# Experts' gate and up rows dealt to the partitions in runs of eight, and a final norm whose factors are computed in groups

## The chip, the cores and the metric

The kernel runs on one core of a Trainium2 chip: TensorE (matmul), VectorE, ScalarE, GpSimd, SyncE (which here only issues transfers) and 16 DMA engines. The metric is the time of one launch on the device, in microseconds (us), as the median of several runs. The profile's short names are PE (TensorE; PEld its weight loads), DVE (VectorE), ACT (ScalarE), POOL (GpSimd) and SP (SyncE); a q behind a name (SPq) is that engine's queue of transfers.

## The reference

One decoder layer over 1024 tokens of width 1024, all in float32: two kinds of attention side by side, a cross-attention into 256 memory tokens, a mixture of 32 experts, a final norm. What matters here is the last third:

```python
def _rms_norm(x, gain):
    y = xf * lax.rsqrt(jnp.mean(xf * xf, axis=-1, keepdims=True) + RMS_EPS)
    return y * gain

def _hierarchical_moe(h, ...):          # h = _rms_norm(x, norm_ffn_g), 1024 x 1024
    # top-1 of 4 groups, then top-2 of its 8 experts, for each token: 2048 assignments
    def block_fn(args):                 # a block of tokens of one expert e
        tok, wt, e = args
        xb = h_pad[tok]
        hidden = jax.nn.silu(xb @ w_gate[e]) * (xb @ w_up[e])   # 1024 -> 256
        return (hidden @ w_down[e]) * wt[:, None]               # 256 -> 1024
    ...
x = x + _hierarchical_moe(...)
return _rms_norm(x, norm_final_g)
```

`w_gate` and `w_up` are [32, 1024, 256], `w_down` is [32, 256, 1024]: an expert has 1 MB of each.

## The kernel before

**The order.** The program's operations are recorded and set in order by a list scheduler written in the kernel (`Sched`), which estimates each operation's cost, gives buffers out and emits one instruction list for each engine before anything runs. All recorded operations are emitted from one place, so nearly every row of the profile carries L481, and rows are told apart by the names of their tiles. Most tiles of 4 KB a partition come from one pool of 50 buffers (`t4`).

**The tokens.** For each of eight tiles of 128 tokens `r_keep` multiplies the residual `xr` by the norm's gain `gb` on GpSimd into `xn`, scales it by the token's factor on ScalarE, and stores it to `XN` in HBM; the residual itself goes to `ACC`. Routing (`r_top`, `r_rank`, `r_index`, `r_weights`) then yields for each expert a list of up to 96 tokens, `gidx`.

**The experts.** `experts` runs over the 32 experts. `moe_piece(e, j)` loads one piece of weights into a tile `eraw`: for j = 0 to 3 two rows of 128 of the 1024 input features, gate beside up, in two transfers of 256 KB (two runs of 1 KB for each partition); for j = 4 and 5 128 rows of `w_down` in one of 512 KB. All are issued by SyncE. `m_split` makes of each tile a rounded part `ehi` (ScalarE) and a rest `elo` (VectorE). `m_x` gathers the expert's 96 rows of `XN` on GpSimd's queue (`xg`) and transposes them, eight blocks of 128 features; `m_gu` multiplies (three matmuls for each block of features: high by high, high by low, low by high); `m_h` and `m_d` make the hidden layer and the down product, and an indirect transfer on GpSimd's queue adds the 96 rows to `ACC`. A row of the contraction, partition q of block k, is feature 128 k + q in both the tokens and the weights. Loads are ordered ahead of their use by two experts (`AHEAD`) and as far as free buffers let the scheduler go.

**Overflow.** For an expert with more than 96 tokens there is a loop (`tc.For_i`) behind a branch, with weights `wgu`, `wdn` of its own; in this run it is not entered.

**The final norm.** For each of eight tiles: load 128 rows of `ACC` into `yt`; square and sum on ScalarE (`sq`, into one column of `ss`); twelve operations on VectorE over that one column (`rsqrt_mean`: scale, bit trick, three Newton steps); one VectorE product of the tile with the factor and the gain; store to `out`. The `ss` tiles come from a pool of four.

Of the kernel before, what the change touches and what calls it, by code (L numbers as in the profile page):

```python
# [12 lines left out]
F32 = mybir.dt.float32  # L13
# [3 lines left out]
AF = mybir.ActivationFunctionType  # L17
OP = mybir.AluOpType
# [4 lines left out]
P = 128  # L23
D = 1024
S = 1024
KT = D // P
NT = S // P
# [28 lines left out]
WHOLE_GU = range(0)  # L56
WHOLE_D = range(4)
WHOLE_PV = ()
TAILV = range(8)
PARK = range(8)  # L60
NPRE = 0
NXG = 3
# [10 lines left out]
NS = 96  # L73
# [442 lines left out]
def hybrid_kernel(ctx: ExitStack, tc: tile.TileContext, a, out):  # L516
    nc = Sched(tc.nc)
    ctx.enter_context(tc.manual_schedule())
    mm = nc.tensor.matmul

    def mm3(o, ah, al, bh, bl, start, stop):
        mm(o, ah, bh, start=start, stop=False)
        mm(o, ah, bl, start=False, stop=False)
        mm(o, al, bh, start=False, stop=stop)

    def sb(stack, name, bufs=1, side="left"):
        return nc.pool(stack, tc, name, bufs, side=side, reuse_waits="tile")
# [3 lines left out]
    sm = sb(ctx, "sm")  # L531
# [14 lines left out]
    def t4(name, *shape, dt=F32):  # L546
        v = big.tile(list(shape) or [P, 1024], dt, tag="t4", name=name, bufs=N4)
        if name == "eraw":
            v.tile.reserve = RESERVE_M
        if name in ("ehi", "elo", "xT", "xw", "hid", "hw", "sg", "y"):  # L550
            v.tile.reserve = RESERVE_W
        return v

    def carve(name):

        t, pos = t4(name), [0]

        def take(*shape, dt=F32):
            n = math.prod(shape) * (2 if dt == BF16 else 4) // 4
            v = t[:, pos[0]:pos[0] + n].bitcast(dt)  # L560
            pos[0] += n
            names = "abc"[:len(shape)]
            return v.rearrange(f"p ({' '.join(names)}) -> p {' '.join(names)}",
                               **dict(zip(names[1:], shape[1:]))) if len(shape) > 1 else v

        return take
# [66 lines left out]
    def rsqrt(dst, v, tmp):  # L633

        nc.vector.tensor_scalar(tmp.bitcast(I32), v.bitcast(I32), 1, None, op0=OP.arith_shift_right)
        nc.vector.tensor_scalar(dst.bitcast(I32), tmp.bitcast(I32), -1.0, 1597463007.0, op0=OP.mult, op1=OP.add)
        for _ in range(3):
            nc.vector.tensor_mul(tmp, dst, dst)
            nc.vector.scalar_tensor_tensor(tmp, tmp, -0.5, v, op0=OP.mult, op1=OP.mult)
            nc.vector.scalar_tensor_tensor(dst, tmp, 1.5, dst, op0=OP.add, op1=OP.mult)  # L640

    def rsqrt_mean(dst, ss, n, tmp):

        nc.vector.tensor_scalar(ss, ss, 1.0 / n, EPS, op0=OP.mult, op1=OP.add)
        rsqrt(dst, ss, tmp)
# [506 lines left out]
    xr = {}  # L1152
# [232 lines left out]
    rt = {}  # L1385
# [46 lines left out]
    def r_keep(t):  # L1432

        x = t4("xn")
        nc.gpsimd.tensor_mul(x, xr[t], rt["gb"])
        nc.scalar.activation(x, x, AF.Copy, scale=rs_[t])
        nc.sync.dma_start(XN[t * P:(t + 1) * P], x)
        nc.sync.dma_start(ACC[t * P:(t + 1) * P], xr[t])
# [170 lines left out]
    w_g, w_u, w_d = (a[n].rearrange("o e d f -> (o e) d f") for n in ("w_expert_gate", "w_expert_up", "w_expert_down"))  # L1609
    pieces = {}  # L1610
# [10 lines left out]
    def moe_piece(e, j):  # L1621

        if e >= NE or (e, j) in pieces:
            return
        raw = pieces[e, j] = t4("eraw", P, 2, 512)
        if j < 4:
            for w, o in ((w_g, 0), (w_u, 256)):
                nc.sync.dma_start(raw[:, :, o:o + 256], w[e, j * 256:(j + 1) * 256].rearrange("(k p) f -> p k f", p=P))
        else:
            nc.sync.dma_start(raw.rearrange("p a c -> p (a c)"), w_d[e, (j - 4) * P:(j - 3) * P])  # L1630

    def moe_load(e):
        for j in range(6):
            moe_piece(e, j)
# [30 lines left out]
    def m_gu(e):  # L1665
        gu = bank()
        for k in range(KT):
            x = st[e]["x"][k // 4]
            sl = slice((k % 4) * NS, (k % 4 + 1) * NS)
            if e in WHOLE_GU:  # L1670
                mm(gu[0:NS], x[:, sl], pieces[e, k // 2][:, k % 2], start=k == 0, stop=k == KT - 1)
            else:
                wh, wl = st[e][k // 2]
                mm3(gu[0:NS], x[:, 0, sl], x[:, 1, sl], wh[:, k % 2], wl[:, k % 2], k == 0, k == KT - 1)
        sg = t4("sg")[:, 0:FF]
        nc.scalar.activation(sg[0:NS], gu[0:NS, 0:FF], AF.Silu)
        nc.vector.tensor_mul(sg[0:NS], sg[0:NS], gu[0:NS, FF:2 * FF])
        st[e]["sg"] = sg
# [141 lines left out]
    lazy, nc = nc, tc.nc  # L1820
    mm = nc.tensor.matmul
# [7 lines left out]
    with tc.If(rnov > 0):  # L1829
# [37 lines left out]
        n = 0  # L1867
# [33 lines left out]
        with tc.For_i(0, rnov, 1) as b:  # L1901
            ev = nc.sync.value_load(bei[0:1, bass.ds(b, 1)], min_val=0, max_val=NE - 1)
            ix = take(1, 2, dt=I32)
            nc.vector.tensor_copy(ix, oidx[:, :, bass.ds(b, 1)].rearrange("p a o -> p (a o)"))
            wx = take(1, 1)
            nc.vector.tensor_copy(wx, ow[:, bass.ds(b, 1)])
            wgu = [r4("wgu", P, 2, 512) for _ in range(4)]
            wdn = [r4("wdn") for _ in range(2)]
            for i in range(4):
                for src, o in ((w_g, 0), (w_u, 256)):  # L1910
                    nc.sync.dma_start(wgu[i][:, :, o:o + 256], src[bass.ds(ev, 1), i * 256:(i + 1) * 256].rearrange(
                        "o (k p) f -> p (o k) f", p=P))
            for i in range(2):
                nc.sync.dma_start(wdn[i], w_d[bass.ds(ev, 1), i * P:(i + 1) * P].rearrange("o p f -> p (o f)"))
            xg = r4("oxg")
            nc.vector.memset(xg, 0.0)
            nc.gpsimd.indirect_dma_start(out=xg, out_offset=None, in_=XN_[:, :],
                                         in_offset=bass.IndirectOffsetOnAxis(ap=ix[:, 1:2], axis=0),
                                         bounds_check=S - 1, oob_is_err=False)
            xT = r4("oxT")  # L1920
            for g in range(2):
                xp = rbank()
                for k in range(4):
                    o = (4 * g + k) * P
                    nc.tensor.transpose(xp[:, k * P:(k + 1) * P], xg[:, o:o + P], ident_)
                nc.vector.tensor_copy(xT[:, g * 512:(g + 1) * 512], xp)
            gu = rbank()
            for k in range(KT):
                mm(gu, xT[:, k * P:(k + 1) * P], wgu[k // 2][:, k % 2], start=k == 0, stop=k == KT - 1)
            sg = take(1, FF)  # L1930
            nc.scalar.activation(sg, gu[:, 0:FF], AF.Silu)
            nc.vector.tensor_mul(sg, sg, gu[:, FF:2 * FF])
            hp = rbank()
            for k in range(2):
                nc.tensor.transpose(hp[:, k * P:(k + 1) * P], sg[:, k * P:(k + 1) * P], ident_)
            hT_ = take(1, 2 * P)
            nc.vector.tensor_copy(hT_, hp[:, 0:2 * P])
            y = r4("oy")
            for n in range(2):
                yp = rbank()  # L1940
                for k in range(2):
                    mm(yp, hT_[:, k * P:(k + 1) * P],
                       wdn[k][:, n * 512:(n + 1) * 512], start=k == 0, stop=k == 1)
                nc.vector.tensor_scalar(y[:, n * 512:(n + 1) * 512], yp, wx, None, op0=OP.mult)
            nc.gpsimd.indirect_dma_start(out=ACC_[:, :], out_offset=bass.IndirectOffsetOnAxis(ap=ix[:, 1:2], axis=0), in_=y,
                                         in_offset=None, bounds_check=S - 1, oob_is_err=False, compute_op=OP.add)
    nc = lazy


    gf = t4("gfin")  # L1950
    nc.sync.dma_start(gf, a["norm_final_g"].partition_broadcast(P))
    y_t = ACC.rearrange("(t p) d -> t p d", p=P)
    o_t = out.rearrange("o (t p) d -> (o t) p d", p=P)
    for t in range(NT):
        y, sq = t4("yt"), t4("sq")
        nc.sync.dma_start(y, y_t[t])
        ss = sm.tile([P, 3], F32, name="ss1", bufs=4)
        nc.scalar.activation(sq, y, AF.Square, accum_out=ss[:, 0:1])
        rsqrt_mean(ss[:, 2:3], ss[:, 0:1], D, ss[:, 1:2])
        if t in TAILV:  # L1960
            nc.vector.scalar_tensor_tensor(y, y, ss[:, 2:3], gf, op0=OP.mult, op1=OP.mult)
        else:
            nc.scalar.activation(y, y, AF.Copy, scale=ss[:, 2:3])
            nc.gpsimd.tensor_mul(y, y, gf)
        nc.sync.dma_start(o_t[t], y)


_INS = ["x", "mem", "positions", "norm_mix_g", "w_in", "diff_lambda_q1", "diff_lambda_k1", "diff_lambda_q2",
# [21 lines left out]
```

## Time and profile before

| | |
|---|---|
| median of 3 runs | 1251.87 us (1247.98 to 1252.53) |
| the profiled execution | 1249.66 us, its span 1247.9 us |
| busy in the span | TensorE 1109.2 us (89%), VectorE 890.9 (71%), ScalarE 802.8 (64%), GpSimd 423.8 (34%) |
| DMA | 256.56 MB in 177,883 packets, 131,058 of them under 2 KB; 206 GB/s over the span |
| granted TensorE clock | 0.936 of full speed, mean |

The span is the time from the first to the last instruction; the profiled execution's own time is 1.8 us longer. Times in the views are counted from the start of the span. Attention and cross-attention end near 740 us, routing near 860, the experts' last scatter is issued at 1215.07, and what follows is the final norm. "Idle before" in a row is the time that the engine stood still ahead of the instruction, with the one that released it. A DMA share of 1.0 means that all 16 engines had a packet under way all the time; in some stretches the packets' times add up to a little more than the engines' time, so that packets of one engine overlap.

### The profile page before, as it was taken

To read this page: it belongs to the slowest core of one execution; us is meant where nothing else is said; L and a number is where in the kernel's file an instruction comes from. 1 tells how busy PE (TensorE), PEld (TensorE's weight loads), DVE (VectorE), ACT (ScalarE), POOL (GpSimd) and SP (SyncE) were. 2 spreads that over 40 slices of the span, in tenths; PEclk is the share of its full clock that TensorE was granted. 3 is DMA by queue.
4 is the path that set the end of the run, shared out by engine and by line. 5 is a ranking of instruction groups with operands and counts; after the bars stand their busy time and mean duration, and the time that the engine had idled before them with its cause. 6 is when DMAs were issued, how large, how long until landed. Compare 5 with 4: busy or idle time off the path is not lost. (4 is left out here: it accounts for less than half of the span.)

```text
span 1247.9 us, 19619 instructions
## 1 busy us (share of the span) xinstructions
PE 1109.2 (89%) x6285; PEld 910.3 (73%) x6285; DVE 890.9 (71%) x2100; ACT 802.8 (64%) x1597; POOL 423.8 (34%) x370
## 2 busy tenths in 40 slices
PE   4999999997888899989999999985999988898980
PEld 3988888895667787778899888874676766566650
DVE  5846535468799979989583466787578877777855
ACT  5744326589787778878372455652677877777862
POOL 2214321169545456847311001242143332121110
PEclk9999999999798998889999999985999999989995
DMA  8028899359745553455441142776899999999967
GB/s 294 19 96 312 309 348 246 109 173 266 170 108 120 133 155 84 123 139 186 169 136 35 34 116 75 272 260 223 271 296 285 299 293 317 312 313 323 322 207 276
DMA packets 177883, 256.56 MB, mean 206 GB/s; under 512 B 17035, under 2 KB 131058, under 8 KB 177778
## 3 DMA queue, kind: packets, MB, share of 16 engines
q1 hardware_dynamic: 161728, 208.22, 54.4%
q0 software_dynamic: 15680, 46.75, 12.3%
q8 instruction: 50, 0.82, 0.3%
q14 instruction: 55, 0.45, 0.1%
q10 hardware_dynamic: 370, 0.32, 0.1%
HBM read 208.57 MB, written 55.05 MB: 211 GB/s over the span
## 5 line engine op out<-in xcount | busy, mean ns | idle before, releaser
L481 DVE TENSOR_TENSOR elo<-eraw,ehi 128x1024 fp32r<-128x1024 f32 x184 | 222.9, 1231 | 54.9 <-ACT ehi L481 53.0
L481 ACT CAST ehi<-eraw 128x1024 fp32r<-128x1024 f32 x184 | 189.3, 1050 | 32.6 <-DMA eraw<-in_w_expert_up_dram 23.8
L481 PE MATMUL bank<-ehi,xT 128*96 128x512 f32 x512 | 178.7, 422 | 19.1 <-ACT y L481 18.3
L481 PE MATMUL bank<-k,q 128*128 128x512 f32 (+5 forms) x480 | 131.4, 381 | 19.4 <-ACT pt L481 7.8
L481 PEld LDWEIGHTS bank<-ehi,xT 128*96 128x96 f32 x512 | 88.2, 172 | 59.4 <-ACT y L481 22.8
L481 DVE TENSOR_TENSOR pT<-bank,pT 128x512 fp32r<-128x512 f32 (+2 forms) x208 | 109.6, 560 | 29.7 <-ACT pT L481 28.9
L481 POOL DMA_INDIRECT ACC<-y,gidx x32 | 54.6, 1707 | 210.9 <-ACT y L481 147.8
L481 PE MATMUL acc<-pT,v 128*128 128x512 f32 (+3 forms) x384 | 114.3, 383 | 10.2 <-DVE pT L481 5.4
L481 ACT CAST pT<-bank 128x512 fp32r<-128x512 f32 (+2 forms) x208 | 93.4, 494 | 33.9 <-PE bank L481 33.0
L481 PE MATMUL bank<-hc,pt 128*128 128x128 f32 x640 | 107.8, 295 | 7.8 <-POOL pt L481 3.6
L481 PEld LDWEIGHTS bank<-k,q 128*128 128x128 f32 (+1 forms) x480 | 84.1, 198 | 37.0 <-DVE mx L481 11.5
L481 PE MATMUL bank<-elo,xT 128*96 128x512 f32 x256 | 106.5, 416 | 2.7 <-DVE elo L481 2.4
L481 PEld LDWEIGHTS bank<-hc,pt 128*128 128x128 f32 x640 | 84.8, 153 | 20.1 <-POOL pt L481 4.2
L481 PE MATMUL lbank<-whi,mix 128*128 128x256 f32 x512 | 96.6, 285 | 0.0
L481 PE MATMUL lbank<-whi,hT 128*128 128x256 f32 (+1 forms) x384 | 86.4, 313 | 0.0
L481 PEld LDWEIGHTS acc<-pT,v 128*128 128x128 f32 x384 | 66.1, 197 | 25.7 <-DVE pT L481 11.3
L481 PE MATMUL lbank<-hT,whi 128*128 128x512 f32 x256 | 81.7, 395 | 0.0
L481 PEld LDWEIGHTS lbank<-whi,mix 128*128 128x128 f32 x512 | 81.2, 192 | 0.1
L481 PE MATMUL bank<-ehi,hid 128*96 128x512 f32 x224 | 75.2, 395 | 1.0 <-ACT hid L481 0.8
L481 DVE TENSOR_REDUCE mx<-bank 128x1 f32<-128x512 f32 (+3 forms) x112 | 61.3, 567 | 15.7 <-PE bank L481 15.5
L481 PE MATMUL lbank<-wlo,mix 128*128 128x256 f32 x256 | 72.5, 283 | 0.0
L481 ACT ACTIVATE pt<-bank,mx 128x512 f32<-128x512 f32 (+2 forms) x96 | 55.3, 583 | 19.7 <-DVE mx L481 18.9
(622 smaller groups left out, 2686.6 us busy)
## 6 DMA issues: line engine op xcount, KB each, us to landing
eraw<-in_w_expert_gate_dram SPq DMA_DIRECT2D x128, 256.0 KB, 5.1
eraw<-in_w_expert_up_dram SPq DMA_DIRECT2D x128, 256.0 KB, 8.7
eraw<-in_w_expert_down_dram SPq DMA_DIRECT2D x64, 512.0 KB, 9.5
k<-KD SPq DMA_DIRECT2D x72, 128.0 KB, 4.1
QM<-st POOLq DMA_DIRECT2D x16, 512.0 KB, 6.6
q<-QM SPq DMA_DIRECT2D x16, 512.0 KB, 4.0
wraw<-in_w_out_dram SPq DMA_DIRECT2D x16, 512.0 KB, 3.5
wraw<-in_w_in_dram SPq DMA_DIRECT2D x12, 512.0 KB, 6.9
```

The costliest lines, as they stand in the source:

```text
L481: getattr(getattr(self.nc, eng), name)(*[real(v) for v in a], **{n: real(v) for n, v in k.items()})
```

## The change

**Gate and up rows.** Partition p now takes the eight rows 8p to 8p + 7 of an expert's gate and up weights, two of them for each j, so that a transfer reads one run of 2 KB for each partition. In the tile, gate stands ahead of up, each with its two rows; `gate_up` gives the matmul the pair (gate row, up row) as its moving operand, 2 x 256 columns with a step between them. The contraction's row, partition q of block k, is now feature 8 q + k, so `r_keep` writes the tokens' columns in that order: GpSimd reads in order and writes groups of eight results 128 columns apart. The overflow loop's rows follow.

**The final norm.** The eight loads are written ahead of the rest, and the factors are computed for the tiles in groups (0), (1, 2), (3, 4), (5, 6, 7): the twelve operations run once for each group over one, two, two and three columns.

```diff
-TAILV = range(8)
+TAIL = ((0,), (1, 2), (3, 4), (5, 6, 7))
...
         x = t4("xn")
-        nc.gpsimd.tensor_mul(x, xr[t], rt["gb"])
+        nc.gpsimd.tensor_mul(x.rearrange("p (k q) -> p q k", k=KT), *[
+            v.rearrange("p (q k) -> p q k", k=KT) for v in (xr[t], rt["gb"])])
         nc.scalar.activation(x, x, AF.Copy, scale=rs_[t])
...
         if j < 4:
-            for w, o in ((w_g, 0), (w_u, 256)):
-                nc.sync.dma_start(raw[:, :, o:o + 256], w[e, j * 256:(j + 1) * 256].rearrange("(k p) f -> p k f", p=P))
+            for i, w in enumerate((w_g, w_u)):
+                nc.sync.dma_start(raw[:, i], w[e].rearrange("(p k) f -> p (k f)", k=KT)[:, j * 512:(j + 1) * 512])
...
+    def gate_up(v, kk):
+        return v.rearrange("p i (k f) -> p k i f", k=2)[:, kk]
...
                 wh, wl = st[e][k // 2]
-                mm3(gu[0:NS], x[:, 0, sl], x[:, 1, sl], wh[:, k % 2], wl[:, k % 2], k == 0, k == KT - 1)
+                mm3(gu[0:NS], x[:, 0, sl], x[:, 1, sl], gate_up(wh, k % 2), gate_up(wl, k % 2), k == 0, k == KT - 1)
...
+    ys = [t4("yt") for _ in range(NT)]
     for t in range(NT):
-        y, sq = t4("yt"), t4("sq")
-        nc.sync.dma_start(y, y_t[t])
-        ss = sm.tile([P, 3], F32, name="ss1", bufs=4)
-        nc.scalar.activation(sq, y, AF.Square, accum_out=ss[:, 0:1])
-        rsqrt_mean(ss[:, 2:3], ss[:, 0:1], D, ss[:, 1:2])
...
+        nc.sync.dma_start(ys[t], y_t[t])
+
+    for tiles in TAIL:
+        n = len(tiles)
+        ss = carve("ss1")(3, n)
+        for i, t in enumerate(tiles):
+            nc.scalar.activation(t4("sq"), ys[t], AF.Square, accum_out=ss[:, 0, i:i + 1])
+        rsqrt_mean(ss[:, 2], ss[:, 0], D, ss[:, 1])
+        for i, t in enumerate(tiles):
+            nc.vector.scalar_tensor_tensor(ys[t], ys[t], ss[:, 2, i:i + 1], gf, op0=OP.mult, op1=OP.mult)
+            nc.sync.dma_start(o_t[t], ys[t])
```

In the order that the scheduler emits, only forms change ahead of the final norm; every instruction of the experts keeps its place. On SyncE's queue, at one pair of gate and up loads, ahead of the first store of a residual (`wraw` are the cross-attention's output weights):

```order
 L481 DMA wraw<-in_w_mem_o_dram 128x2x512 x2
-L481 DMA eraw<-in_w_expert_gate_dram 128x2x256
-L481 DMA eraw<-in_w_expert_up_dram 128x2x256
+L481 DMA eraw<-in_w_expert_gate_dram 128x512
+L481 DMA eraw<-in_w_expert_up_dram 128x512
 L481 DMA ACC<-xr_6782 128x1024
```

Nothing moved; each transfer has one run a partition in place of two. On GpSimd, at the last of the products for `xn` (`rtmp` are the routing's, `xg` the buffers that the gathers fill):

```order
 L481 TENSOR_TENSOR rtmp_9504<-A,w_9490 128x384 x2
-L481 TENSOR_TENSOR xn<-xr_7414,gb 128x1024
-L481 TENSOR_TENSOR xn<-xr_7417,gb 128x1024
+L481 TENSOR_TENSOR xn<-xr_7414,gb 128x128x8
+L481 TENSOR_TENSOR xn<-xr_7417,gb 128x128x8
 L481 MEMSET xg 128x1024 x3
```

Again only the form differs. On VectorE, in the final norm (`ss` with a number is one group's columns); before, at the second product of a tile:

```order
L481 TENSOR_TENSOR ss_13626<-ss_13626 128x1
L481 TENSOR_SCALAR ss_13636<-ss_13636 128x1
L481 SCALAR_TENSOR_TENSOR yt<-yt,ss_13614,gfin 128x1024
L481 SCALAR_TENSOR_TENSOR ss_13626<-ss_13626 128x1
L481 TENSOR_TENSOR ss_13636<-ss_13636 128x1
L481 TENSOR_SCALAR ss_13653<-ss_13653 128x1
```

and with the change, from the end of the second group on:

```order
L481 SCALAR_TENSOR_TENSOR yt<-yt,ss_13614,gfin 128x1024 x2
L481 TENSOR_SCALAR ss_13630<-ss_13630 128x2 x2
L481 TENSOR_TENSOR ss_13630<-ss_13630 128x2
L481 SCALAR_TENSOR_TENSOR ss_13630<-ss_13630 128x2 x2
L481 TENSOR_TENSOR ss_13630<-ss_13630 128x2
L481 SCALAR_TENSOR_TENSOR ss_13630<-ss_13630 128x2 x2
```

Operations of two or three tiles alternated; now one group's stand behind each other, with 48 of them in place of 96.

## Rows read from the trace of the kernel before

**Rows 1.** The page: busy TensorE (us, share, instructions); DMA busy tenths in 40 slices.

```profile
PE 1109.2 (89%) x6285; PEld 910.3 (73%) x6285; DVE 890.9 (71%) x2100; ACT 802.8 (64%) x1597; POOL 423.8 (34%) x370
...
DMA  8028899359745553455441142776899999999967
```

**Rows 2.** Table by stage: length, busy us of PE PEld DVE ACT POOL, clock, DMA share, GB/s.

```profile
878.00:1008.00 130.00, 127.02 (x604) 86.72 (x603) 100.83 (x118) 100.70 (x149) 42.85 (x28) 0.99 1.00 298
1008.00:1150.00 142.00, 122.78 (x553) 85.33 (x552) 105.45 (x120) 104.64 (x145) 32.61 (x24) 0.93 1.01 313
1150.00:1200.00 50.00, 47.47 (x203) 31.28 (x201) 41.82 (x48) 40.92 (x59) 8.02 (x5) 0.97 1.03 328
```

**Rows 3.** Who waited for whom in 1008 to 1200: us, times, longest us.

```profile
ACT ehi L481 <- DMA eraw<-in_w_expert_up_dram: 23.8, 20, 2.8
ACT ehi L481 <- DMA eraw<-in_w_expert_down_dram: 6.2, 28, 0.3
```

**Rows 4.** Timeline of GpSimd: start us, us, instruction; idle before and its releaser.

```profile
887.96 1.52 POOL L481 DMA_INDIRECT ACC<-y,gidx  x1 [8.34 <-ACT hw L481]
...
1008.27 2.33 POOL L481 DMA_INDIRECT ACC<-y,gidx  x1 [5.05 <-ACT hid L481]
...
1149.51 1.71 POOL L481 DMA_INDIRECT ACC<-y,gidx  x1 [9.33 <-ACT y L481]
```

**Rows 5.** DMA view: packets of 878 to 1200, then of 1008 to 1200.

```profile
DMA packets 72631, 99.49 MB, mean 309 GB/s; under 512 B 6977, under 2 KB 62200, under 8 KB 72607
...
DMA packets 44825, 60.80 MB, mean 317 GB/s; under 512 B 4061, under 2 KB 38667, under 8 KB 44810
```

**Rows 6.** DMA view: 693.6 to 695 (query weights), 719.6 to 720.8 (output weights), 835 to 838 (experts).

```profile
DMA packets 541, 0.54 MB, mean 384 GB/s; under 512 B 16, under 2 KB 541, under 8 KB 541
...
q1 hardware_dynamic: 541, 0.54, 108.7%
...
DMA packets 254, 0.49 MB, mean 406 GB/s; under 512 B 16, under 2 KB 16, under 8 KB 254
...
q1 hardware_dynamic: 254, 0.49, 104.9%
...
DMA packets 1076, 1.04 MB, mean 348 GB/s; under 512 B 63, under 2 KB 1075, under 8 KB 1075
```

**Rows 7.** GpSimd's groups (busy us, mean ns) in 740 to 870, and timeline there.

```profile
L481 POOL TENSOR_TENSOR xn<-xr,gb 128x1024 f32<-128x1024 f32 x8 | 19.2, 2396 | 53.5 <-issue 23.7 <-DVE xr L481 18.5 <-DMA eraw<-in_w_expert_up_dram 8.3
...
L481 POOL TENSOR_TENSOR wr<-wr,gcol 128x288 f32<-128x288 f32 x1 | 1.2, 1153 | 47.0 <-PE lbank L481 47.0
...
792.90 2.37 POOL L481 TENSOR_TENSOR wlo<-wraw,whi 128x1024 fp32r<-128x1024 f32 x1 [6.98 <-ACT whi L481]
...
818.33 2.41 POOL L481 TENSOR_TENSOR xn<-xr,gb 128x1024 f32<-128x1024 f32 x1 [3.09 <-ACT hr L481]
...
824.17 1.66 POOL L481 TENSOR_TENSOR rtmp<-A,w 128x384 bf16<-128x384 bf16 x2 [2.27 <-DVE w L481]
...
836.46 2.36 POOL L481 TENSOR_TENSOR xn<-xr,gb 128x1024 f32<-128x1024 f32 x1 [8.29 <-DMA eraw<-in_w_expert_up_dram]
...
847.73 1.15 ACT L481 ACTIVATE xn<-xn,fs 128x1024 f32<-128x1024 f32 x1 [5.17 <-issue]
```

**Rows 8.** Timeline of the final norm: SyncE's loads, then VectorE.

```profile
1220.61 4.02 SPq L481 DMA_DIRECT2D yt<-ACC  x8
...
1225.64 0.53 DVE L481 TENSOR_SCALAR ss<-ss 128x1 f32<-128x1 f32 x3 [16.38 <-ACT sq L481]
...
1227.95 1.28 DVE L481 SCALAR_TENSOR_TENSOR yt<-yt,ss,gfin 128x1024 f32<-128x1024 f32 x1
...
1240.78 1.28 DVE L481 SCALAR_TENSOR_TENSOR yt<-yt,ss,gfin 128x1024 f32<-128x1024 f32 x1
1241.98 0.15 DVE L481 TENSOR_TENSOR ss<-ss 128x1 f32<-128x1 f32 x1
...
1242.56 1.28 DVE L481 SCALAR_TENSOR_TENSOR yt<-yt,ss,gfin 128x1024 f32<-128x1024 f32 x1
```

More of the change, by code (lines that the diff above doesn't have):

```diff
@@ L1670, in m_gu @@
             if e in WHOLE_GU:
-                mm(gu[0:NS], x[:, sl], pieces[e, k // 2][:, k % 2], start=k == 0, stop=k == KT - 1)
+                mm(gu[0:NS], x[:, sl], gate_up(pieces[e, k // 2], k % 2), start=k == 0, stop=k == KT - 1)
             else:
                 wh, wl = st[e][k // 2]
-                mm3(gu[0:NS], x[:, 0, sl], x[:, 1, sl], wh[:, k % 2], wl[:, k % 2], k == 0, k == KT - 1)
+                mm3(gu[0:NS], x[:, 0, sl], x[:, 1, sl], gate_up(wh, k % 2), gate_up(wl, k % 2), k == 0, k == KT - 1)
         sg = t4("sg")[:, 0:FF]
@@ L1910, in hybrid_kernel @@
                 for src, o in ((w_g, 0), (w_u, 256)):
-                    nc.sync.dma_start(wgu[i][:, :, o:o + 256], src[bass.ds(ev, 1), i * 256:(i + 1) * 256].rearrange(
-                        "o (k p) f -> p (o k) f", p=P))
+                    nc.sync.dma_start(wgu[i][:, :, o:o + 256], src[bass.ds(ev, 1)].rearrange(
+                        "o (p k) f -> p (o k) f", k=KT)[:, 2 * i:2 * i + 2])
             for i in range(2):
@@ L1953, in hybrid_kernel @@
     o_t = out.rearrange("o (t p) d -> (o t) p d", p=P)
+    ys = [t4("yt") for _ in range(NT)]
     for t in range(NT):
-        y, sq = t4("yt"), t4("sq")
-        nc.sync.dma_start(y, y_t[t])
-        ss = sm.tile([P, 3], F32, name="ss1", bufs=4)
-        nc.scalar.activation(sq, y, AF.Square, accum_out=ss[:, 0:1])
-        rsqrt_mean(ss[:, 2:3], ss[:, 0:1], D, ss[:, 1:2])
[L1960 to L1965, printed above, removed]
+        nc.sync.dma_start(ys[t], y_t[t])
[8 more added lines that the diff above has]
+            nc.sync.dma_start(o_t[t], ys[t])
 _INS = ["x", "mem", "positions", "norm_mix_g", "w_in", "diff_lambda_q1", "diff_lambda_k1", "diff_lambda_q2",
```

## The prediction

> **What bounds the kernel now.** I read the page first, then a table by stage, then who waited for whom in the last third, then the DMA queues of the same stretch. On the page TensorE is busy 89% of the span, which says little, since its busy time is modelled; the DMA line is the one to look at: its last sixteen slices stand at 9 nearly throughout, the middle of the span at 1 to 5 [rows 1]. The table by stage puts that in numbers [rows 2]. From 878 to 1200 us, the experts, the DMA share is 1.00 to 1.03 in all three rows, while VectorE and ScalarE work about three quarters of the time (105.45 and 104.64 of 142 us in the middle row). So the sixteen DMA engines have no idle time there.
>
> A full DMA share alone doesn't make DMA the bound; somebody has to starve. In 1008 to 1200 us ScalarE, which makes the high part of every weight tile, waits 23.8 us for the up weights and 6.2 us for the down weights to land [rows 3]; the same view of 878 to 1008 has no such row. The pace agrees [rows 4]: between the scatters at 887.96 and 1008.27 lie twelve experts, 10.0 us each; from there to 1149.51 twelve more, 11.8 us each. So up to about 1008 the kernel lives on tiles loaded ahead and runs at the engines' pace, and from there at the DMA's. Whatever shortens the DMA work of this stage moves its end, by up to the 30.0 us that ScalarE starves.
>
> **Part one: 2 KB packets for gate and up.** A gate or up transfer of 256 KB now reads 128 runs of 2 KB where it read 256 of 1 KB; bytes, number and order of transfers stay. In 878 to 1200 us there are 62200 - 6977 = 55,223 packets of 1 KB, 56.5 MB; 38667 - 4061 = 34,606 of them, 35.4 MB, in the starved part from 1008 [rows 5]. Nearly all are gate and up.
>
> What a packet of either size costs is seen where one kind runs alone [rows 6]. 1 KB packets of the query weights of the cross-attention: 384 GB/s; 2 KB packets of that block's output weights: 406 GB/s. The same rows give the occupied time of a packet: 108.7% of 16 engines over 1.4 us, less 16 short ones, over 525 packets is 46 ns; 104.9% over 1.2 us and 238 packets is 84 ns. A pair goes from 92 to 84 ns. The two readings differ, because occupied times overlap (they add up to 108.7% of the engines' time), and more so with 1 KB. The third row is the experts' own 1 KB packets alone: 348 GB/s, slower than the query weights', so there may be more to gain.
>
> Four prices follow. By rate, whole stage: 56.5 MB at 384 is 147.3 us, at 406 139.3, a gain of 8.0 us. By rate, starved part alone (if the tiles freed earlier can't be used before 1008): 92.3 to 87.3, 5.0 us. By occupied time, 8 ns a pair over 16 engines: 27,600 pairs give 13.8 us, the 17,300 of the starved part 8.7 us. From the experts' own 348 to 406 GB/s: 162.5 to 139.3, 23 us, the far end. I take **-9 us**: the second reading of the starved part and the first of the whole stage both lie within 1 us of it. For the transfers before 878 I count nothing: no row of that stretch shows ScalarE waiting for them.
>
> The matmuls now read their moving operand as two runs of 256 columns instead of one of 512. No row shows such an operand; TensorE is not what the others wait for in the starved part, and a loss must first use up the difference between 10.0 and 11.8 us an expert. I price it at 0, and at up to +2 in the range. ScalarE's and VectorE's splits work on the whole tile and don't change.
>
> **Part two: the permuted token rows.** GpSimd's product that makes `xn` writes each group of eight results 512 B apart; it takes 2.396 us now, eight times [rows 7]. Such an output isn't in the trace. The nearest rows: contiguous 2.3 ns an element; the router product with a broadcast operand, 1.153 us for 288 elements, 4.0 ns. So 2.4 to 4.1 us. Even 1.7 us more each is covered: after the first four the queue was idle 6.98 us before the `wlo` at 792.90 (they would add 6.8); behind the one at 818.33 the queue idled 2.27 us ahead of 824.17, more than the 1.7; the last, from 836.46, would end at 840.6, and ScalarE scales its result at 847.73. Cost 0.
>
> **Part three: the final norm.** Its title says that all loads are issued first; in the row of SyncE the eight loads already go out in one run from 1220.61, so nothing is gained there [rows 8]. What changes is VectorE, which is busy without a break from 1225.64 to 1243.84 (18.2 us) and sets the end. Now, eight short chains of 12 one-column operations are interleaved: the first takes 1225.64 to 1227.95, 2.31 us or 0.19 each, since each waits for the one ahead; the other 84, mixed, fill what remains: 18.2 - 2.31 - 8 x 1.20 (the step from 1240.78 to 1241.98) = 6.3 us, 0.075 each. After: four chains, 48 operations, but the order no longer mixes them (three of the 48 are slipped between others). 45 x 0.19 = 8.7, plus 8 x 1.20 = 9.6, is 18.3 us. Half the operations, each at the full latency: **+0.1 us**. Both ends: were the chains after the first at 0.075, the tail would gain 33 x 0.12 = 3.9 us; if the burst of three stores at the end queues, it loses 0.5.
>
> **The sum.** -9 + 0 + 0.1 = -8.9 us. The profiled execution took 1249.66 us, span 1247.9; after it 1240.8. It ran 2.2 us below the median of 1251.87, so the median after is 1251.87 - 8.9 = **1243.0 us**.
>
> **Rivals.** *Little comes through.* In the stage a packet doesn't run alone: gathers and scatter-adds of 4 KB rows run among the loads, and the whole moves 298 to 328 GB/s [rows 2] where 1 KB packets alone reach 384. If what holds the packets there is the traffic (bytes, shared ports of the tiles) and not their own fixed cost, only part of the 5.0 us of the starved part is left: 2 to 5 us, 1247 to 1250. For it: that gap of rates. Against it: a DMA share of 1.0 means that engines are occupied by packets, and a fixed cost per packet is part of it. The Trainium skill stands near this rival: "DMA: Bandwidth & Descriptors", section "Why small descriptors are slow", has about 3 cycles fixed per packet and calls joining worth it only for descriptors of 256 B and less. By its figures a pair goes from 2 x 35 to 67 beats, 4.3%, an estimate of 6.3 us on 147.3; the trace's 384 to 406 is 5.4%, so the size agrees and the verdict "only at 256 B" doesn't decide here.
>
> *Slower: the new addresses.* Before, one transfer reads 256 KB without a gap; now each of 128 partitions reads 2 KB of every 8 KB. That addresses matter is in the rows: two streams of equal 1 KB packets run at 384 and at 348 GB/s [rows 6]. The break-even is a rate of 2 KB packets equal to that of the present 1 KB ones. If they fall from 384 to 348, 56.5 MB cost 15 us more: 1267. Against it: the query weights are read with gaps too (1 KB of every 2 KB) and are the faster of the two.
>
> *Slower: GpSimd.* If the strided product costs more than 847.73 - 836.46 = 11.3 us, the last rows of tokens come late, and routing and the first gather with them; beyond this each us costs at least one, and 25 us would turn the gain into a loss (1257). Ten times the contiguous cost; hardly likely.
>
> **How the numbers follow.** What a measurement of this kernel can tell from no change is about 0.5%, 6.3 us: faster is below 1245.6, slower above 1258.1. My forecast, a gain of 6.3 us or more (1229 to 1245.6), has 0.60; little comes through (1245.6 to 1251) 0.28; the addresses 0.08 and GpSimd 0.04, a quarter of both still inside 0.5%. That gives faster 0.60, same 0.31, slower 0.09. The range leaves out the two slow cases and the far end of the 23 us: 1235 to 1252.
>
> **What will show it.** Right: packets under 2 KB fall from 131,058 by about 65,500 and 32,800 of 2 KB take their place; in 1008 to 1200 ScalarE's waits for weights fall from 30.0 to about 20 us; the middle pace falls from 11.8 toward 11.2 us an expert; the DMA share stays at 1.0 and its rate rises; the last scatter issues about 9 us earlier; the products `xn` take 2.4 to 4.1 us with ScalarE's scaling where it was; VectorE's tail lasts 18 us again, with 48 short operations. Wrong: DMA share unchanged with the rate unchanged (traffic binds, not packets), gate and up transfers that take longer to land (addresses), starvation gone and the pace at 10 us (then the gain is nearer 20), or a tail of 15 us.

## The result, and the profile after

The changed kernel takes 1244.38 us (median of 8 runs, 1242.64 to 1246.35), the kernel before 1251.78 beside it: a ratio of 0.9945, 95% interval 0.9924 to 0.9965. Measured a second time with the experiments it was 1242.44 us and 0.9939 (0.9916 to 0.9962). It is 7 us faster, 0.55%, a little more than the 0.5% that can be told; the interval reaches down to 0.35%. The forecast of 1243.0 holds as a number. The experiments show that its working doesn't: the loads give less than it says, and a part of the diff to which it gave no gain at all gives the rest.

The profiled execution took 1243.66 us, span 1241.9 (before 1249.66 and 1247.9). The page of after: the busy line, the DMA line in 40 slices, and the packets of the whole span.

```profile
PE 1106.9 (89%) x6285; PEld 907.8 (73%) x6285; DVE 887.9 (71%) x2052; ACT 800.4 (64%) x1597; POOL 429.5 (35%) x370
...
DMA  8028898359744453445541132767799999999967
...
DMA packets 145115, 256.56 MB, mean 207 GB/s; under 512 B 17035, under 2 KB 65522, under 8 KB 145010
```

VectorE runs 2052 instructions, 48 fewer than in [rows 1]. The page before counted 131,058 packets under 2 KB, this one 65,522. The table by stage of after (columns as in [rows 2]):

```profile
878.00:1008.00 130.00, 124.52 (x585) 84.19 (x584) 98.80 (x116) 97.57 (x145) 42.46 (x27) 0.99 0.97 306
1008.00:1150.00 142.00, 128.52 (x596) 88.42 (x595) 111.62 (x130) 109.48 (x155) 36.40 (x24) 0.96 0.98 317
1150.00:1200.00 50.00, 45.74 (x197) 28.94 (x196) 41.30 (x46) 40.36 (x55) 8.45 (x5) 1.00 0.95 308
```

The DMA share is no longer 1.00 and 1.01 but 0.97 and 0.98 in the first two rows, and the rate has hardly risen (306 and 317 GB/s, where it was 298 and 313). The last row (0.95, 308 GB/s) doesn't compare, because the loads end within it, and 6 us earlier than before. The last two loads of after, then of before:

```profile
1188.09 1.00 SPq L481 DMA_DIRECT2D eraw<-in_w_expert_down_dram  x2
```

```profile
1194.53 1.15 SPq L481 DMA_DIRECT2D eraw<-in_w_expert_down_dram  x2
```

Who waited in 1008 to 1200, as in [rows 3], and four scatters of GpSimd's timeline as in [rows 4]: the first, the thirteenth, the 25th and the last; then the last of before:

```profile
ACT ehi L481 <- DMA eraw<-in_w_expert_up_dram: 20.7, 17, 3.0
ACT ehi L481 <- DMA eraw<-in_w_expert_down_dram: 4.8, 13, 1.2
```

```profile
887.19 1.52 POOL L481 DMA_INDIRECT ACC<-y,gidx  x1 [8.34 <-ACT hw L481]
...
1010.80 2.17 POOL L481 DMA_INDIRECT ACC<-y,gidx  x1 [5.26 <-ACT hid L481]
...
1142.99 1.71 POOL L481 DMA_INDIRECT ACC<-y,gidx  x1 [9.34 <-ACT y L481]
...
1208.90 1.42 POOL L481 DMA_INDIRECT ACC<-y,gidx  x1 [4.57 <-DMA ACC<-y,gidx]
```

```profile
1215.07 1.42 POOL L481 DMA_INDIRECT ACC<-y,gidx  x1 [4.71 <-DMA ACC<-y,gidx]
```

ScalarE waits 25.5 us for up and down weights, not 30.0. Twelve experts in the middle take 1142.99 - 1010.80 = 132.2 us, 11.0 each, where they took 141.2; the first twelve 123.6, where they took 120.3. The last scatter comes 6.17 us earlier, and the span is 6.0 us shorter: all of the gain lies ahead of the final norm. There, as in [rows 8], SyncE's loads and VectorE's first and last operations:

```profile
1214.25 3.95 SPq L481 DMA_DIRECT2D yt<-ACC  x8
```

```profile
1219.16 0.53 DVE L481 TENSOR_SCALAR ss<-ss 128x1 f32<-128x1 f32 x3 [15.93 <-ACT sq L481]
...
1221.47 1.28 DVE L481 SCALAR_TENSOR_TENSOR yt<-yt,ss,gfin 128x1024 f32<-128x1024 f32 x1
...
1225.04 2.48 DVE L481 SCALAR_TENSOR_TENSOR yt<-yt,ss,gfin 128x1024 f32<-128x1024 f32 x2
...
1233.96 3.68 DVE L481 SCALAR_TENSOR_TENSOR yt<-yt,ss,gfin 128x1024 f32<-128x1024 f32 x3
```

VectorE's stretch is 1219.16 to 1237.64, 18.48 us (before 18.20), its first chain 2.31 us, as before. The gate and up matmuls of before and of after in 878 to 1200, and GpSimd's product of after in 740 to 870:

```profile
L481 PE MATMUL bank<-ehi,xT 128*96 128x512 f32 x485 | 168.4, 420 | 19.1 <-ACT y L481 18.3
```

```profile
L481 PE MATMUL bank<-ehi,xT 128*96 128x512 f32 x493 | 166.2, 409 | 8.0 <-ACT y L481 6.8
```

```profile
L481 POOL TENSOR_TENSOR xn<-xr,gb 128x1024 f32<-128x1024 f32 x8 | 19.3, 2412 | 53.5 <-issue 23.7 <-DVE xr L481 18.4 <-DVE rper L481 8.3
```

A gate and up matmul on the two-run operand takes 409 ns where one run took 420, and `xn` in the strided order 2412 ns (2396 in [rows 7]). Neither costs anything that these rows show.

One more number serves all that follows: how long the sixteen DMA engines are occupied for a megabyte of SyncE's queue (q1) in 878 to 1200 us. The DMA view gives packets, MB and share; 81.1% of 322 us over 84.49 MB is 3.09 us per MB before, 77.0% over 85.03 MB is 2.92 after.

```profile
q1 hardware_dynamic: 66335, 84.49, 81.1%
```

```profile
q1 hardware_dynamic: 38855, 85.03, 77.0%
```

### The profile page after: what moved, and what is told of

It reads as the page before. It is cut to its first block, busy times and chain, and to the rows that moved or that the text cites. A ratio compares the mean times of both kernels' runs of the same rounds, so it can differ in the third digit from the quotient of the medians.

```text
span 1241.9 us, 19564 instructions
## 1 busy us (share of the span) xinstructions
PE 1106.9 (89%) x6285; PEld 907.8 (73%) x6285; DVE 887.9 (71%) x2052; ACT 800.4 (64%) x1597; POOL 429.5 (35%) x370
## 5 line engine op out<-in xcount | busy, mean ns | idle before, releaser
L481 ACT CAST ehi<-eraw 128x1024 fp32r<-128x1024 f32 x184 | 188.5, 1050 | 29.1 <-DMA eraw<-in_w_expert_up_dram 20.7
L481 PE MATMUL bank<-ehi,xT 128*96 128x512 f32 x512 | 174.0, 412 | 8.0 <-ACT y L481 6.8
L481 PE MATMUL bank<-k,q 128*128 128x512 f32 (+5 forms) x480 | 131.3, 381 | 18.3 <-ACT pt L481 7.8
L481 PEld LDWEIGHTS bank<-ehi,xT 128*96 128x96 f32 x512 | 85.7, 167 | 46.9 <-ACT y L481 11.1
L481 PEld LDWEIGHTS lbank<-whi,mix 128*128 128x128 f32 x512 | 81.1, 191 | 0.1
```

The costliest lines, as they stand in the source:

```text
L481: getattr(getattr(self.nc, eng), name)(*[real(v) for v in a], **{n: real(v) for n, v in k.items()})
```

## The experiments

Times are medians; the ratio is to the kernel before, run beside each (1251.78 us beside after; 1251.25 beside rows_only to rows_512, 1250.53 beside tail_again to half_down, 1251.13 beside the last four). "Middle twelve" is the time between the thirteenth and the 25th scatter, "experts" that between the first and the last.

| kernel | time, us | ratio, 95% interval | q1, us per MB | middle twelve | experts |
|---|---|---|---|---|---|
| before | 1251.78 | 1 | 3.09 | 141.2 | 327.1 |
| after | 1244.38 | 0.9945 (0.9924 to 0.9965) | 2.92 | 132.2 | 321.7 |
| rows_only | 1245.93 | 0.9954 (0.9936 to 0.9971) | 2.95 | 134.5 | 322.8 |
| tail_only | 1245.88 | 0.9955 (0.9932 to 0.9978) | 3.03 | 137.7 | 323.9 |
| rows_1k | 1249.72 | 0.9997 (0.9984 to 1.0011) | 3.07 | 140.8 | 325.3 |
| rows_512 | 1286.19 | 1.0286 (1.0252 to 1.0320) | 3.52 | 153.2 | 360.6 |
| tail_again | 1246.28 | 0.9965 (0.9950 to 0.9980) | 3.04 | 136.5 | 323.0 |
| after_again | 1242.44 | 0.9939 (0.9916 to 0.9962) | 2.91 | 135.1 | 318.5 |
| align | 1242.34 | 0.9941 (0.9921 to 0.9960) | 2.91 | 128.9 | 319.3 |
| half_down | 1221.19 | 0.9779 (0.9745 to 0.9813) | 2.96 | 113.7 | 295.3 |
| before_moved | 1246.33 | 0.9959 (0.9944 to 0.9975) | 3.04 | 139.5 | 324.1 |
| tail_kept | 1250.71 | 0.9997 (0.9982 to 1.0011) | 3.11 | 140.8 | 329.3 |
| best | 1248.21 | 0.9976 (0.9965 to 0.9987) | 2.90 | 129.5 | 319.3 |
| rows_4k | 1233.99 | 0.9867 (0.9850 to 0.9884) | 2.74 | 124.8 | 308.1 |

### Each part of the change alone

**rows_only** is the changed kernel with the old final norm:

```diff
-    ys = [t4("yt") for _ in range(NT)]
-    ... (grouped factors)
+    for t in range(NT):
+        y, sq = t4("yt"), t4("sq")
+        nc.sync.dma_start(y, y_t[t])
+        ss = sm.tile([P, 3], F32, name="ss1", bufs=4)
+        ... (as in the kernel before)
```

> The gate and up rows in runs of eight with the final norm of before. Packet theory: the whole gain lies in the experts' stage, because 65,536 fewer packets pass through DMA engines that have no idle time there; this kernel gains 6 to 7.5 us on the kernel before (1244.3 to 1246), within 1 us of the changed kernel. Rival, the final norm carries a share: this kernel gains under 5 us. VectorE's stretch of the final norm about 18.2 us as before.

**tail_only** is the kernel before with the new final norm (the same diff the other way round).

> The grouped final norm with the experts' loads of before. Packet theory: no difference, between -1 and +0.5 us; VectorE's stretch of the final norm 18.3 to 18.6 us against 18.2, because half as many one-column operations each pay the whole latency. Rival, the final norm carries a share of the gain: 2 us or more faster.

The rows alone are worth 0.46%, 5.8 us of 1251; that is a little under what was expected. VectorE's stretch of the final norm is 19.0 us there (1221.27 to 1240.29), not 18.2, with the instructions of before: from trace to trace it differs by most of a microsecond. The final norm alone was to do nothing, and is worth 0.45%, 5.6 us. Its trace contradicts the name: the last scatter, then VectorE's first and last operation in the final norm of tail_only:

```profile
1213.41 1.42 POOL L481 DMA_INDIRECT ACC<-y,gidx  x1 [4.51 <-DMA ACC<-y,gidx]
```

```profile
1223.03 0.53 DVE L481 TENSOR_SCALAR ss<-ss 128x1 f32<-128x1 f32 x3 [15.22 <-ACT sq L481]
...
1238.21 3.67 DVE L481 SCALAR_TENSOR_TENSOR yt<-yt,ss,gfin 128x1024 f32<-128x1024 f32 x3
```

VectorE takes 1223.03 to 1241.88, 18.85 us, more than the 18.20 of before. From the last scatter to the end it is 1246.1 - 1213.41 = 32.7 us, and before 1247.9 - 1215.07 = 32.8. What is gained lies in the experts (323.9 us, not 327.1), whose code is word for word that of before. Either it was chance, or the edit does something else.

**tail_again** and **after_again** are tail_only and the changed kernel once more, side by side.

> The grouped final norm alone, timed a second time, because its first time (5 us faster) doesn't fit its trace, where VectorE's stretch of the final norm is longer than before (18.85 against 18.20 us) and everything that is gained lies ahead of the final norm, in code that is the same as before. If that gain was chance between runs: 1248 to 1252 us, and less than 2 us from the kernel before. If it is real: again 4 to 6 us faster.

> The changed kernel a second time beside it, on the same chip. Packet theory: 1243 to 1246 us; the distance to tail_again is then what the rows in runs of eight are worth, 5 to 7 us. If the final norm carries the gain: within 2 us of tail_again.

It is no chance: 0.35% (0.20 to 0.50), with the experts at 323.0 us. That the final norm carries all falls too: after_again is 3.8 us ahead of tail_again (some 2 us either way, by the spread of the runs), less than the 5 to 7 that were expected.

### What the final norm's edit does: it moves the tiles

The old final norm took its factors from four small tiles of their own (`sm.tile([P, 3], F32, name="ss1", bufs=4)`); the new one cuts them from a 4 KB tile (`carve("ss1")`). The small tiles lie ahead of the fifty 4 KB tiles. In the built program each takes 32 bytes, and without them the lowest 4 KB tile begins at byte 24416 of a partition, not 24544: every tile, those of the experts' weights among them, lies 128 bytes lower.

**before_moved** leaves the final norm's order as it was and only takes its factors from 4 KB tiles; **tail_kept** has the new final norm and a pad that puts the tiles back where they were.

```diff
(before_moved, against before)
-        ss = sm.tile([P, 3], F32, name="ss1", bufs=4)
+        ss = t4("ss1")[:, 0:3]
(tail_kept, against tail_only)
+    pad = sm.tile([P, 32], F32, name="pad")
+    nc.gpsimd.memset(pad, 0.0)
     gains = early(P)
```

> The kernel before, order and loads untouched, but the final norm's small factor tiles are cut from 4 KB tiles, as in the changed kernel, so that all 4 KB tiles lie 128 bytes lower in the on-chip memory. The final norm alone timed 4 to 5 us faster twice, while its stretch in the traces, from the last scatter to the end, is no shorter (32.7 and 33.4 us against 32.8). If the place of the tiles gives that gain: 1245 to 1247.5 us. If the final norm gives it: 1249.5 to 1252.

> The grouped final norm alone again, with a pad of 128 bytes ahead of the 4 KB tiles, so that these lie where they lie in the kernel before. If the place of the tiles gives the gain of tail_only: 1249.5 to 1252 us, as before. If the grouped final norm gives it: 1245 to 1247.5 us.

Both come out as the place says, and as the final norm doesn't: 0.9959 with the old order on moved tiles, 0.9997 with the new order on tiles left in place. So the grouped final norm is worth nothing (0.9997 against 1, 0.9955 and 0.9965 against 0.9959), and 128 bytes are worth about 5 us. Where they act is in the DMA view of 878 to 1200, q1 of before_moved and of tail_kept:

```profile
q1 hardware_dynamic: 65808, 84.61, 80.0%
```

```profile
q1 hardware_dynamic: 65603, 83.29, 80.4%
```

The engines are occupied 80.0% of 322 us for 84.61 MB, 3.04 us per MB, and 80.4% for 83.29 MB, 3.11. All three kernels with 1 KB packets of the old addresses on moved tiles stand at 3.03 to 3.04, both on tiles in the old place at 3.09 and 3.11. It is the same transfers and the same matmuls; only the byte at which a tile begins differs.

The Trainium skill has a rule that points here: "DMA: Bandwidth & Descriptors", section "How a descriptor splits into AXI transactions", lets a transaction start only at a multiple of 256 B, so that a descriptor that starts off one pays for bytes it doesn't use; its own example starts 224 bytes past. 24544 is 224 past a multiple of 256, 24416 is 96 past. By that count a packet of 1 KB takes 39 beats in the old place and 35 in the new, an estimate of 10%; the rows show 2%, so the direction agrees and the size doesn't, and the page tells it of reads, where these packets write into tiles. No run here had tiles at a multiple of 256.

**align** moves all tiles of the changed kernel by another 32 bytes, to 24448.

```diff
+    pad = sm.tile([P, 8], F32, name="pad")
+    nc.gpsimd.memset(pad, 0.0)
     gains = early(P)
```

> The changed kernel with every 4 KB tile 32 bytes further in the on-chip memory (a pad of 32 bytes ahead of them), so that tiles begin at a multiple of 128 bytes; before and after they begin 32 bytes past a multiple of 64. The changed final norm gave up small tiles, and so moved all tiles by 128 bytes too. If the place of the tiles matters to the packets: over 3 us apart from after_again. If not: within 1.5 us of it.

1242.34 against 1242.44 us, 2.91 us per MB in both: no difference, though the runs of align spread from 1237 to 1249 us, so that the times alone would miss one of up to 3. So a further shift neither helps nor harms, and the multiple of 128 brings nothing. Two starts (24416, 24448) are good, one (24544) is 2% worse; what law lies behind this stays open.

### Packets or addresses

**rows_1k** has the new row order and its addresses, but lands each row by itself; **rows_512** cuts each row in two.

```diff
(rows_1k)
-   nc.sync.dma_start(raw[:, i], w[e].rearrange("(p k) f -> p (k f)", k=KT)[:, j * 512:(j + 1) * 512])
+   nc.sync.dma_start(raw[:, :, i * 256:(i + 1) * 256],
+                     w[e].rearrange("(p k) f -> p k f", k=KT)[:, 2 * j:2 * j + 2])
(rows_512)
+   nc.sync.dma_start(raw.rearrange("p k (h i f) -> p (k h) i f", h=2, i=2)[:, :, i],
+                     w[e].rearrange("(p k) (h f) -> p (k h) f", k=KT, h=2)[:, 4 * j:4 * j + 4])
```

> The changed kernel's row order (eight rows of an expert to a partition, permuted token columns) and its addresses, but each row of 1 KB lands in the tile as a packet of its own, as before, and the matmul operand is one run of 512 columns again. Packet theory: the gain is gone, 1250 to 1253 us, about 131,000 packets under 2 KB, ScalarE's waits for the up and down weights near 30 us again in the last 200 us. Rival, the gain is in the order of the addresses: 1243 to 1247 us with 1 KB packets. Rival, the new addresses cost something that the packets hide: over 1255 us.

> The same addresses, the rows cut into 512 B packets (four for each 2 KB packet of the changed kernel; the matmul operand in four runs of 128 columns). Packet theory with a fixed cost of 8 ns a packet (46 ns for 1 KB, 84 ns for 2 KB): 65,536 packets more than before over 16 engines are 33 us of engine time, all of it in a stage that is starved already, so about 1265 to 1285 us, and ScalarE's waits for weights in the last 200 us at least doubled. Rival, bytes and not packets hold the engines: below 1258 us.

q1 of both in 878 to 1200, and ScalarE's wait of rows_512 in 1008 to 1200:

```profile
q1 hardware_dynamic: 66412, 84.57, 80.7%
```

```profile
q1 hardware_dynamic: 107171, 74.66, 81.6%
```

```profile
ACT ehi L481 <- DMA eraw<-in_w_expert_up_dram: 40.1, 19, 3.6
```

On the same tiles and the same addresses, packets of 512 B, 1 KB and 2 KB occupy the engines for 3.52, 3.07 and 2.92 us per MB and give 1286, 1250 and 1244 us (1242 the second time). The packet's size acts, as the theory says, but not as a fixed cost alone: that would halve the saving with each doubling, and the steps are 0.45, 0.15 and, in rows_4k below, 0.18 us per MB. rows_512 lands just above the 1265 to 1285 that were expected; its wait for the up weights, 40.1 us, isn't double the 30.0 of [rows 3]. Its matmuls, on four runs, take 431 ns, so that a part of its 36 us over the kernel before may be TensorE's.

rows_1k met its number (to 0.3 us), but for two reasons that cancel. Its tiles are moved ones, so without the new order it would be at about 1246 (tail_only, tail_again, before_moved). It is some 4 us slower (1249.72 against the 1245.88 of tail_only beside it): with packets of 1 KB the new order does cost something (3.07 against 3.04 us per MB), as the rival on addresses said; the packets of 2 KB then win 5 to 7 us.

### Is DMA the bound, and how far?

**half_down** leaves out the down weights of every second expert:

```diff
         raw = pieces[e, j] = t4("eraw", P, 2, 512)
+        (ahead of it)  if j > 3 and e % 2: pieces[e, j] = pieces[e - 1, j]; return
```

> The changed kernel in which every second expert doesn't load its down weights and uses those of the expert ahead of it (it leaves out 16 of 32 loads of 1 MB, a sixth of the bytes of the stage, and so computes another output). Theory that DMA is the bound of the last stretch: starvation is gone, every expert goes at the engines' pace of about 10 us, ScalarE's waits for weights fall from 25 to under 8 us, and the time to about 1222 to 1232. Rival, TensorE or the chain from gather to scatter is next right behind: under 6 us of gain.

Who waited of ScalarE in 878 to 1180 (the whole answer), and the middle stage:

```profile
ACT y L481 <- PE bank L481: 29.2, 38, 1.7
ACT sg L481 <- PE bank L481: 21.0, 18, 6.8
ACT sg L481 <- ACT ehi L481: 6.1, 10, 0.9
```

```profile
1008.00:1150.00 142.00, 140.43 (x679) 98.81 (x678) 128.84 (x151) 124.55 (x183) 35.59 (x27) 1.00 0.95 305
```

No row of ScalarE names a weight any more. Each expert takes 113.7 / 12 = 9.5 us, TensorE is busy 140.43 of 142 us at a granted clock of 1.00 (2.4 GHz; it was 0.93 in [rows 2]), and the kernel gains 21 us more (1221.19 us, just under the 1222 to 1232 expected). So in the changed kernel the loads still hold the middle stretch, and TensorE is next behind them, at 9.5 us an expert. The version leaves out transfers as well as bytes; the two weren't separated.

### Further on: two versions

**best** puts another final norm on the changed kernel.

```diff
-TAIL = ((0,), (1, 2), (3, 4), (5, 6, 7))
+TAIL = ((0, 1), (2, 3, 4), (5, 6, 7)); TAILP = (3, 4, 6)
+    zs = {t: t4("yz") for t in TAILP}
+    for t in TAILP:
+        nc.gpsimd.tensor_mul(zs[t], ys[t], gf)
...
+            if t in TAILP:
+                nc.scalar.activation(zs[t], zs[t], AF.Copy, scale=ss[:, 2, i:i + 1])
+                nc.sync.dma_start(o_t[t], zs[t])
```

> The changed kernel with another final norm: three groups of factors (36 one-column operations on VectorE, not 48), and for three of the eight tiles GpSimd multiplies by the gain while the squares run, and ScalarE multiplies by the factor; VectorE has five wide products left. VectorE's stretch: 36 x 0.195 + 5 x 1.2 = 13 us, with waits about 15, instead of 18.5 to 19. Expected: the last scatter to the end takes 29 to 30 us, not 33, and the time is 1239 to 1241.5 us. Rival, GpSimd's products slow VectorE or the stores queue: over 1242.

The rival holds. GpSimd's and VectorE's timelines in the final norm:

```profile
1224.30 8.98 POOL L481 TENSOR_TENSOR yz<-yt,gfin 128x1024 f32<-128x1024 f32 x3 [12.19 <-DVE ss L481]
```

```profile
1224.19 4.58 DVE L481 SCALAR_TENSOR_TENSOR yt<-yt,ss,gfin 128x1024 f32<-128x1024 f32 x2
1228.69 4.81 DVE L481 TENSOR_SCALAR ss<-ss 128x3 f32<-128x3 f32 x3
...
1237.58 0.58 DVE L481 TENSOR_SCALAR ss<-ss 128x3 f32<-128x3 f32 x3 [0.98 <-ACT sq L481]
```

While GpSimd multiplies (1224.30 to 1233.28), VectorE's two products take 4.58 us where the two at 1225.04 of after take 2.48, and three operations of three columns take 4.81 us; the same three take 0.58 at 1237.58, when GpSimd is done. Together they take 9.3 us (1224.19 to 1233.50), near the 10.3 that it would be one after the other: three products of 2.396 us on GpSimd ([rows 7]) and 3.1 us on VectorE. ScalarE's eighth square, too, starts only at 1236.42, behind a scaling that had to wait for VectorE's factors. From the last scatter (1210.69) to the end it is 37.1 us, 4 more than after.

**rows_4k** carries the rows further: four to a packet, gate and up in tiles of their own, and the matmuls of gate and up in two halves of 256 columns.

```diff
-            for i, w in enumerate((w_g, w_u)):
-                nc.sync.dma_start(raw[:, i], w[e].rearrange("(p k) f -> p (k f)", k=KT)[:, j * 512:(j + 1) * 512])
+            w = (w_g, w_u)[j // 2]
+            nc.sync.dma_start(raw.rearrange("p a c -> p (a c)"),
+                              w[e].rearrange("(p k) f -> p (k f)", k=KT)[:, j % 2 * 1024:(j % 2 + 1) * 1024])
...
+        for i in range(2):
+            for k in range(KT):
+                mm3(gu[0:NS, i * 256:(i + 1) * 256], x[:, 0, sl], x[:, 1, sl], wh, wl, k == 0, k == KT - 1)
```

> The changed kernel with gate and up rows in runs of four to a packet: 16,400 packets of 4 KB in place of 32,800 of 2 KB, six transfers of 512 KB for an expert, not ten; the price is on TensorE, whose gate and up matmuls read 256 columns at a time and are twice as many. Packet theory with the same fixed cost: half of what the step from 1 KB gave, 2 to 4 us faster than the changed kernel (1239 to 1242). Rival, TensorE becomes the bound: its busy time from 878 to 1150 rises and the time is 1246 or more.

```profile
878.00:1008.00 130.00, 125.46 (x907) 108.39 (x906) 97.12 (x115) 97.63 (x145) 38.47 (x28) 0.99 0.96 318
1008.00:1150.00 142.00, 135.28 (x968) 119.67 (x967) 119.57 (x140) 116.39 (x167) 34.48 (x25) 0.98 0.98 331
```

```profile
ACT ehi L481 <- DMA eraw<-in_w_expert_gate_dram: 4.8, 4, 1.6
ACT ehi L481 <- DMA eraw<-in_w_expert_up_dram: 2.8, 4, 1.7
ACT ehi L481 <- DMA eraw<-in_w_expert_down_dram: 1.5, 4, 0.8
```

```profile
q1 hardware_dynamic: 23472, 85.47, 72.8%
```

1233.99 us, 1.33% under the kernel before and 8 to 10 us under the changed one: it beats both, by at least twice what was expected. ScalarE waits 9.1 us for weights in 1008 to 1200, and q1 needs 2.74 us per MB. The fear for TensorE was empty here: in 878 to 1008 it runs 907 matmuls where after has 585, at 125.46 us busy against 124.52, and the first twelve experts take 122.5 us against 123.6; the weight loads rise to 108.39 us, beside them. Whether the second matmul costs time where TensorE alone sets the pace, as in half_down, no run shows. The version also makes six transfers of an expert's weights where there were ten, each of 512 KB, and gate arrives whole ahead of up; how much of the gain comes from that and how much from the packets was not separated.

## Why the prediction was right in its number and not in its sum

**The bound: right.** half_down takes a sixth of the weights' bytes away, and ScalarE's waits for them and 21 us of time go with them. One reading ahead of it was too bold: of the last sixteen digits of the page's DMA line nine are a 9, not nearly all. The table by stage carries the argument.

**The term of the loads, -9 us: too large.** Alone, in the place the tiles had, the rows give 5.8 us (3.6 to 8.0 by the interval). Of the four prices worked out, the lowest, the rate in the starved part (5.0 us), is the nearest, and the step that failed is the choice between them: "the second reading of the starved part and the first of the whole stage both lie within 1 us of it" averaged over readings that don't measure the same. The occupied time of rows_only did fall nearly as priced; q1 of it in 878 to 1200:

```profile
q1 hardware_dynamic: 38875, 84.94, 77.7%
```

That is 2.95 us per MB, not 3.09: 12 us over the 84.5 MB of the stretch, where the price was 13.8. But only about half of it became time. From 1008 to 1150 the DMA share of after is 0.98 where it was 1.01, and the rate 317 GB/s where it was 313: a part of what was freed is now idle time of the engines. "The DMA share stays at 1.0 and its rate rises" is therefore wrong in its first half, and right by 1 to 3% in its second. ScalarE's waits fell to 25.5 us, not 20, and with the rows alone hardly at all (24.7 and 5.1 us in rows_only, though its time fell); the last scatter came 6.2 us earlier, not 9, and that with both parts of the change.

What the loads of after wait for is in the trace too. SyncE's queue in 878 to 1008, then in 1008 to 1200:

```profile
SPq L481 <- PE bank L481: 15.9, 13, 5.2
SPq L481 <- DMA ACC<-y,gidx: 10.6, 2, 7.9
```

```profile
SPq L481 <- DMA eraw<-in_w_expert_gate_dram: 43.4, 59, 2.8
SPq L481 <- DMA eraw<-in_w_expert_up_dram: 38.8, 56, 3.0
SPq L481 <- DMA eraw<-in_w_expert_down_dram: 30.6, 29, 3.1
```

In the first stretch the queue stands 26.5 us until TensorE or a scatter is done, so that loads can't run further ahead there; this fits the price that counted the starved part alone. In the second it waits 112.8 us for earlier transfers of its own (before 101.3) and for the other engines only 3.4 us (before 20.7). In the built program SyncE's transfers use eight semaphores in turn, so that each waits until the one eight ahead of it has landed. rows_4k's transfers of 512 KB put more bytes under way in those eight. Whether that, rather than the packet, makes rows_4k gain more than the step to 2 KB was not tested, so why so little came through stays open.

**The final norm, +0.1 us: right for what it priced, and blind to the rest.** Its own stretch is 18.48 us where 18.3 was forecast (18.8 to 19.4 in the other traces with this order), with 48 operations fewer, and tail_kept shows that the edit by itself is worth nothing (0.9997). But it gave up four small tiles, moved all others by 128 bytes and gained 5 us in the experts. No term of the sum and no rival had this. It can be read in the diff, since `ss1` leaves its pool; its price could not, as all packets of before land in one place only.

**The sum.** -8.9 was made of -9 and 0.1. Alone, the measured parts are -5.8 (rows) and -5 (place), and together -6.9 and -7.6 by the two ratios: they fall short of their sum by about 3, which is hardly more than the intervals leave open. On moved tiles the rows come out at 3.8 us (after_again against tail_again), which the spread doesn't tell from the 5.8 in the old place. The occupied time points to a real overlap: the place takes off 0.05 to 0.08 us per MB with 1 KB packets, but only 0.03 to 0.04 with 2 KB (2.95 in rows_only, 2.92 and 2.91 in after). A term too large by 3 and a missing one of 5, less an overlap of about 3, came close to the total. That the number held is luck to that extent.

**The rivals.** *Little comes through* had 2 to 5 us for the loads. The loads alone come out inside it on moved tiles (3.8) and just above it in the old place (5.8), both well under the 9 of the forecast. The runs save 13% of the engines' time per MB of the queue from 512 B to 1 KB, 5% from 1 KB to 2 KB, and from 2 KB to 4 KB, with fewer transfers, another 6%, though a third of the bytes, the down weights, keep their packets. The Trainium skill's verdict beside this rival ("DMA: Bandwidth & Descriptors", section "Why small descriptors are slow": worth it only at 256 B and less) is on joining descriptors into packets; here the runs themselves grew longer, and for that the trace doesn't agree (13%, 5%, 6%). *The new addresses* exist, as a cost of some 4 us with 1 KB packets on moved tiles, far under the 15 that were feared, and the packets outweigh them. *GpSimd* never came near: `xn` takes 2412 ns.

**What held:** 65,536 packets under 2 KB fewer; a middle pace of 11.0 us an expert, 11.3 the second time (toward 11.2); `xn` at the lower bound of 2.4 to 4.1 us; the matmul's two-run operand at nothing (409 ns where it was 420).

## What to carry to other kernels

A gain in a stage that DMA bounds is to be read from the stage's own rate, not from the packets' occupied time: this kernel turned 12 us of engine time into 6. An edit that adds or frees a small tile moves everything behind it; where transfers bind, hold the tiles in place with a pad before a difference is put down to the edit itself, and cross the two (edit with and without, place old and new) as tail_only, tail_kept and before_moved do. If longer packets help, go on until the row of the waits is empty: 4 KB, with fewer and larger transfers, gave more than the step to 2 KB, and twice as many matmuls cost no time that can be seen. Look also at what the loads' own queue waits for, before the packets are blamed for all of it.

## What was not expected of the hardware

- The place of the tiles: with the same transfers, 1 KB packets occupy the engines 3.03 to 3.04 us per MB into tiles that start at byte 24416 and 3.09 to 3.11 at 24544, 5 us of 1251.
- GpSimd's product of three tiles holds VectorE up: two products take 4.58 us instead of 2.48, three operations of three columns 4.81 instead of 0.58.
- A product on GpSimd whose results go out 512 B apart costs hardly more than one in a row: 2412 against 2396 ns.
- Gate and up matmuls of 256 columns, twice as many, cost no time that can be seen here: 125.46 against 124.52 us busy in 130 us, with the weight loads (108.39 us) beside them.
